# A diffusion block on one core: recurrence units of four channel tiles instead of two, a root taken from the tanh of the half angle, sums of squares moved to ScalarE

## Chip, cores and metric

The kernel runs on one core of a Trainium2 chip. The metric is the device time of one execution in microseconds; the time shown is the median of three runs. A kernel of this kind has five engines that run side by side, each with its own queue of instructions: TensorE (PE, matrix products), VectorE (DVE), ScalarE (ACT), GpSimd (POOL) and SyncE (SP, which here only issues DMA transfers).

## What is computed

A block of width 1024 over 2048 tokens: a mixing phase, a projection with a residual, and a convolutional feed-forward part. The change touches the mixing phase alone. Cut to what matters:

```python
a_r = sigmoid(block_diag(xa, w_a) + b_a)          # 8 heads of 64x64, xa: 512 channels
i   = sigmoid(block_diag(xa, w_x) + b_x)
a   = exp(-8 * a_r * softplus(-lam))
b   = sqrt(1 - a*a) * (i * xa)
h[t] = a[t] * h[t-1] + b[t]                       # forward, and once more backward
ya = gelu(z_gate) * (h_f + h_b)                   # 512 channels
yb = pool_group(z_pool)                           # 256 channels
yc = gmlp_group(z_uv)                             # 256 channels
mix = concat(ya, yb, yc) @ w_out                  # then rmsnorm, gate, residual
out = conv_ffn(...)                               # 1024 -> 5632, 3x3 conv, -> 1024
```

The first states of both directions come from the same recurrence over 256 context tokens.

## The kernel before

Channels lie on the partitions. The 512 recurrent channels are four channel tiles of 128 (the sets P and Q hold two each), the 2048 tokens four chunks of 512. Large products are done in half precision as high and low part, three matmuls for each of eight slices of depth (`mm3`, L356 to L361), so one projection of a channel tile and chunk is 24 matmuls of 128x512. In the trace they are called by what they make: `xa` (input of the recurrence), `gt` (its output gate), `pl` (pooling branch), `uv` (gMLP branch).

A recurrence unit (`lru_units`, L506) takes one direction, one chunk and two channel tiles. For each tile `coeffs` (L440 to L451) issues two f32 matmuls with a 128x128 block-diagonal weight (`rp` L443, `ip` L444; two heads of 64x64 lie on the diagonal, the rest is zero), two sigmoids and a tanh on ACT. `coeffs2` (L453) takes the exponential on ACT, then `combine` (L459 to L463) the square of it and i\*xa on POOL and (q+1)\*t on DVE. `coeffs3` (L465) takes the square root on ACT, `finish_b` (L471 to L473) multiplies on POOL, and `scan` (L475 to L479) runs the recurrence on DVE. So a unit crosses from ACT to POOL and DVE, back to ACT for the root, to POOL, and to DVE. The tiles `lru` hold four arrays of 512 columns and have two buffers. ACT loads a table before each change of function set (`act`, L133 to L141, keeps the sets from mixing).

Forward results are stored to memory (`hfd`, `keep_f` L517). Backward units read them back (`hf`, one buffer) and POOL adds both (`join`, L520 to L523). `gates` (L640 to L648) then applies the gelu of `gt`, multiplies on DVE (L647) and sums squares on DVE (`vsumsq`, L153). `pool_br` (L539) issues `pl`, a chain of DVE adds on tiles `pa` and `pb` and a small f32 matmul `pp` (L535). `gmlp` (L598 to L638) issues `uv`, a normalisation on DVE and POOL, the matmuls `sp` (L623) and the transposes `tp` (L632). `wout_stats` (L684) reads w_out once (`ro`) and sums its squares on DVE; `prep_out` (L695) reads it again (`ro2`) and splits it on DVE into high and low part (L312, L313) for the `wo` matmuls (L878). `mods` (`wm`, L660) makes further modulation rows on DVE.

The order of all this is written by hand: each word of the string `ORDER` (L38 to L43) calls one step, its first letter chosen from the table `run` (L771 to L784): x normalises the next chunk, c is the context recurrence, a the projection `xa`, f and b the recurrence forward and backward, G the gates, g and p one step of gMLP and pooling, m of `wm`, w of w_out, i prepares slots of w_in, L opens the pool of late tiles. A scheduler sorts each engine's instructions by its own estimate of time, with the order of the calls as priority; each engine then runs its list in order.

## Time and profile before

| | |
|---|---|
| median of three runs | 2157.3 us (2153.7 to 2160.75) |
| the profiled execution's own time | 2155.6 us |
| its span | 2153.8 us |
| busy: PE, DVE, ACT, POOL | 2022.0 (94%), 1593.2 (74%), 1194.6 (55%), 610.1 (28%) us |
| mean granted TensorE clock | 0.972 |

The page lists busy time for each engine, 40 equal slices of the span, the DMA queues, the chain of work that ended last (each step followed back to what released it), the costliest groups of instructions and the DMA issues. Below, four further views of the same execution are used: stretches of the span with the busy time of each engine, what an engine waited for, groups of instructions by line and shape, and single instructions in order of time.

### The profile page before, as it was taken

Reading aid. Unit: us, or ns where it says so; the run is one execution under the profiler, and the core shown is the slowest. Engines: PE = TensorE matmul, PEld = TensorE weight load, DVE = VectorE, ACT = ScalarE, POOL = GpSimd, SP = SyncE. Lnnn points to the kernel's source line nnn. Section 1 sums busy time; section 2 is a strip of 40 time slices with the busy share of each in tenths; the row PEclk is TensorE's granted clock in tenths of the full one; section 3 lists DMA queues with packets and bytes.
Section 4 is the critical chain, followed back from the end, with each engine's and each line's share of the span. In section 5 each row is a group of like instructions: output and inputs, shape, how many; then the busy total and the mean of one; then the engine's idle time right before and its main releaser. Section 6 shows DMA issues by size and latency. Waiting matters only on the chain.

```text
span 2153.8 us, 24277 instructions
## 1 busy us (share of the span) xinstructions
PE 2022.0 (94%) x9215; PEld 933.4 (43%) x9215; DVE 1593.2 (74%) x2214; ACT 1194.6 (55%) x1665; POOL 610.1 (28%) x457
## 2 busy tenths in 40 slices
PE   6878989788899998999999999999999999999995
PEld 1433444333455443444444444444444444444442
DVE  5687788999655359978667776867777686777876
...
GB/s 297 183 88 74 69 166 89 180 35 85 135 136 114 79 64 20 130 66 132 89 117 98 79 124 72 108 78 102 94 88 100 74 103 88 100 95 69 40 157 156
DMA packets 73480, 224.78 MB, mean 104 GB/s; under 512 B 7442, under 2 KB 18066, under 8 KB 68498
## 3 DMA queue, kind: packets, MB, share of 16 engines
...
## 4 chain that ended last, share of the span: by engine, by line
PE 55%; DVE 3%; POOL 1%; DMA 1%; ACT 1%; issue 1%; POOLq 0%; SPq 0%; DVEq 0%; ACTq 0%
PE up L359 12%; PE up L360 12%; PE up L361 12%; PE dn L1054 6%; PE dn L1056 6%; PE dn L1055 6%; DVE cv L1011 2%; DMA hT<-accd 1%; POOL hT L1069 0%; DVE hT L1086 0%; DVE hT L1060 0%; DMA wm<-in_wmT_dram 0%; POOL fms L159 0%; PE sct L121 0%; POOL out_dram L1087 0%
## 5 line engine op out<-in xcount | busy, mean ns | idle before, releaser
L1011 DVE SCALAR_TENSOR_TENSOR cv<-z,cols,cv 128x1008 f32<-128x1008 f32 (+3 forms) x704 | 870.4, 1250 | 276.6 <-ACT cv L1005 188.7
L359 PE MATMUL up<-hT,uw 128*128 128x512 f16 x1408 | 534.1, 379 | 2.6 <-ACT z L846 2.6
L361 PE MATMUL up<-hT,uw 128*128 128x512 f16 x1408 | 534.1, 379 | 0.0
L360 PE MATMUL up<-hT,uw 128*128 128x512 f16 x1408 | 534.1, 379 | 0.0
L1071 POOL DMA_DIRECT2D accd<-dd x132 | 114.2, 865 | 704.1 <-ACT dd L1065 697.9
L846 ACT ACTIVATE z<-up,upinv 128x512 f32<-128x512 f32 x176 | 120.5, 685 | 311.2 <-PE up L361 310.8
L1065 ACT ACTIVATE dd<-dn,gdi 128x512 f32<-128x512 f32 x320 | 214.2, 680 | 115.0 <-PE dn L1056 107.5
L1054 PE MATMUL dn<-dw,gs 128*128 128x512 f16 x704 | 267.2, 380 | 7.1 <-ACT dd L1065 5.3
L1055 PE MATMUL dn<-dw,gs 128*128 128x512 f16 x704 | 267.5, 380 | 0.0
L1056 PE MATMUL dn<-dw,gs 128*128 128x512 f16 x704 | 265.8, 380 | 0.0
L360 PEld LDWEIGHTS <-uw 128*128 128x128 f16 x1408 | 137.8, 98 | 167.5 <-issue 3.6
L359 PEld LDWEIGHTS <-uw 128*128 128x128 f16 x1408 | 139.0, 99 | 164.7 <-issue 0.6
L361 PEld LDWEIGHTS <-uw 128*128 128x128 f16 x1408 | 137.8, 98 | 166.5 <-issue 0.6
L832 POOL TENSOR_TENSOR uw<-ur,uw 128x2048 f16<-128x2048 f32 x22 | 89.5, 4070 | 168.9 <-ACT ur L831 168.9
L135 ACT ACT_TABLE_LOAD x77 | 98.8, 1283 | 47.4 <-PE rp L443 28.8
L1005 ACT ACTIVATE cv<-z,cols 128x1024 f32<-128x1024 f32 x88 | 106.0, 1206 | 2.0
L1055 PEld LDWEIGHTS <-gs 128*128 128x128 f16 x704 | 68.8, 98 | 86.8 <-issue 9.5
L1054 PEld LDWEIGHTS <-gs 128*128 128x128 f16 x704 | 72.2, 103 | 78.8 <-issue 0.8
L1056 PEld LDWEIGHTS <-gs 128*128 128x128 f16 x704 | 68.9, 98 | 83.5 <-issue 0.6
L986 POOL TENSOR_TENSOR dw<-dr,dw 128x1024 f16<-128x1024 f32 x22 | 46.4, 2127 | 141.8 <-PE dn L1056 100.3
L150 ACT ACTIVATE junk<-g 128x1024 bf16<-128x1024 f32 x44 | 46.3, 1053 | 59.9 <-DVE g L1019 59.9
L878 PE MATMUL wo<-wo,ysp 128*128 128x512 f16 x256 | 77.1, 383 | 1.0 <-ACT gm L807 1.0
...
## 6 DMA issues: line engine op xcount, KB each, us to landing
...
ur<-in_wup_dram SPq DMA_DIRECT2D x22, 1024.0 KB, 5.6
...
hT<-in_wm_dram SPq DMA_DIRECT2D x8, 1024.0 KB, 14.4
xt<-in_xT_dram SPq DMA_DIRECT2D x8, 1024.0 KB, 7.1
...
```

What stands on the lines that cost most here:

```text
L135: ins = A.activation(out_, in_, func, **kw).ins
L359: T.matmul(ps, wh(k), hh(k), start=(k == 0), stop=False)
L360: T.matmul(ps, wh(k), hl(k), start=False, stop=False)
L361: T.matmul(ps, wl(k), hh(k), start=False, stop=(k == KT - 1))
L846: A.activation(z[:, ab, b * 8:(b + 1) * 8, :], ps.rearrange("p (r x) -> p r x", x=64), AF.Identity, scale=upinv[:, c:c + 1])
L1005: A.activation(t, z[:, ab, r0:r0 + 16, :].rearrange("p r x -> p (r x)"), AF.Identity, bias=col("fcb", c + NP * ab), scale=wt(0, 0))
L1011: V.scalar_tensor_tensor(o, z[:, ab, ya + dy:yb + dy, xa + dx:xb + dx], wt(dy, dx), o, op0=OP.mult, op1=OP.add)
L1054: T.matmul(ps[h], hi, wh, start=i == 0, stop=False)
L1055: T.matmul(ps[h], hi, wl, start=False, stop=False)
L1056: T.matmul(ps[h], lo, wh, start=False, stop=i == n - 1)
L1065: A.activation(d[:, h * CH:(h + 1) * CH], ps[h], AF.Copy, scale=di)
L1071: G.dma_start(accd[t], d, accum_op=OP.add)
```

## The change

Seven edits. (1) A recurrence unit takes all four channel tiles (set A); the table tile `lru` holds three arrays and has four buffers, in a pool of its own. (2) The root is taken from the tanh of the half: with t = tanh(4pr) and a = exp(-8pr), sqrt(1-a\*a) = (1+a)\*sqrt(t). So ACT does sigmoids, tanh, exp and sqrt without waiting for POOL or DVE between them; POOL and DVE follow (i\*xa, (a+1)\*i, i\*sqrt); the square of a on POOL is gone. (3) Each gate matmul of 128x128 becomes two of 64x64 that use the upper and lower half of the partitions of input and output; the weight is loaded by eight transfers of 64x4x64 instead of one of 128x4x4x128. (4) The sums of squares of `gg`, `pa` and `ro` go from DVE to ACT (`sumsq`, L149). (5) The split of w_out goes from DVE (two instructions) to ACT (two) and POOL (one) (`split_ag`, L315 to L319 before). (6) gMLP's output is written over the tile it came from, `gg` has two buffers, not three. (7) `ORDER` is new, with one step F (`fold_ffn`) that ran after the mixing phase before.

Program instructions from before to after: gate matmuls 64 of 128x512 and 16 of 128x256 to 128 of 64x512 and 32 of 64x256; ACT table loads 77 to 44; DVE 2120 to 2073, ACT 1479 to 1494, POOL 462 to 430, SP 312 to 319.

```diff
 ORDER = """
-x1 cP g g cQ x2 a1P f0P a1Q g a2P f0Q x3 g f1P a2Q g f1Q a3P g f2P L a3Q m6
-g i89 f2Q g g i45 m6 f3P g g g g f3Q g g g m6 i67 m6 b3P p p p p
-m6 b3Q G3P p m6 w4 b2P G3Q p m6 w4 b2Q G2P p m6 w2 b1P G2Q p m6 w2 b1Q G1P p
-m6 w2 b0P G1Q m6 w2 b0Q G0P m9 G0Q w9 w9
+x1 cA g g g x2 a1P a1Q f0A g g x3 a2P a2Q f1A g g g a3P a3Q f2A L g g i89 m6 f3A g g g g i45 m6 g g g m6 i67 m6
+b3A p p p G3P m6 p p G3Q m6 w4 b2A p p p p G2P m6 w4 G2Q m6 w2 b1A m6 w2 G1P m6 w2 G1Q m6 w2 F b0A w2 G0P G0Q w9 w9
 """
...
-    gwt = mix.tile([128, 4, 4, 128], F32, name="gwt")
+    gwt = mix.tile([128, 4, 4, 64], F32, name="gwt")
+    HALVES = (slice(0, 64), slice(64, 128))
...
+        V.tensor_scalar(lam, p, -4.0, None, op0=OP.mult)
...
+    def lru_tile(name):
+        return lrup.tile([128, 3, CH], F32, tag="lru", name=name)
...
-        T.matmul(rp[:, :w], gwt[:, j, 2 * d, :], xa, start=True, stop=True)
-        T.matmul(ip[:, :w], gwt[:, j, 2 * d + 1, :], xa, start=True, stop=True)
-        c = lru_tile([128, 4, CH], F32, "lru") if c is None else c
-        r, i, t, q = (c[:, a, :] for a in range(4))
-        act(r[:, :w], rp[:, :w], AF.Sigmoid, bias=col("ba", 4 * d + j))
-        act(i[:, :w], ip[:, :w], AF.Sigmoid, bias=col("bx", 4 * d + j))
-        k = klam[:, 4 * d + j:4 * d + j + 1]
-        act(t[:, :w], r[:, :w], AF.Tanh, scale=k)
-        return r, i, t, q, k
-
-    def coeffs2(cs, xas, w):
-        for c in cs:
-            act(c[0][:, :w], c[0][:, :w], AF.Exp, scale=c[4])
-        for c, xa in zip(cs, xas):
-            combine(c, xa, w)
-
-    def combine(c, xa, w):
-        r, i, t, q, k = c
-        G.tensor_tensor(q[:, :w], r[:, :w], r[:, :w], op=OP.mult)
-        G.tensor_tensor(i[:, :w], i[:, :w], xa, op=OP.mult)
-        V.scalar_tensor_tensor(t[:, :w], q[:, :w], 1.0, t[:, :w], op0=OP.add, op1=OP.mult)
-
-    def coeffs3(cs, w):
-        for c in cs:
-            act(c[2][:, :w], c[2][:, :w], AF.Sqrt, scale=-1.0)
-        for c in cs:
-            finish_b(c, w)
-
-    def finish_b(c, w):
-        i, t = c[1], c[2]
-        G.tensor_tensor(i[:, :w], i[:, :w], t[:, :w], op=OP.mult)
+        for ps, g in ((rp, 2 * d), (ip, 2 * d + 1)):
+            for h in HALVES:
+                T.matmul(ps[h, :w], gwt[h, j, g, :], xa[h], start=True, stop=True)
+        c = lru_tile("lru") if c is None else c
+        r, i, t = (c[:, a, :w] for a in range(3))
+        act(r, rp[:, :w], AF.Sigmoid, bias=col("ba", 4 * d + j))
+        act(i, ip[:, :w], AF.Sigmoid, bias=col("bx", 4 * d + j))
+        act(t, r, AF.Tanh, scale=col("lam", 4 * d + j))
+        return r, i, t, klam[:, 4 * d + j:4 * d + j + 1]
+
+    def coeffs2(cs, xas):
+        for r, i, t, k in cs:
+            act(r, r, AF.Exp, scale=k)
+        for r, i, t, k in cs:
+            act(t, t, AF.Sqrt, scale=-1.0)
+        for (r, i, t, k), xa in zip(cs, xas):
+            G.tensor_tensor(i, i, xa, op=OP.mult)
+            V.scalar_tensor_tensor(i, r, 1.0, i, op0=OP.add, op1=OP.mult)
+            G.tensor_tensor(i, i, t, op=OP.mult)
 
...
-        ts = [lru_tile([128, 4, CH], F32, "lrc") for j in js]
+        ts = [lru_tile("lrc") for j in js]
         cs = [coeffs(j, d, xac[0][:, j, :], LC, ts[j - js[0]][:, :, d * LC:(d + 1) * LC]) for j, d in jd]
-        coeffs2(cs, [xac[0][:, j, :] for j, d in jd], LC)
-        coeffs3(cs, LC)
+        coeffs2(cs, [xac[0][:, j, :] for j, d in jd])
         for (j, d), c in zip(jd, cs):
-            q = c[3]
+            q = c[2]
...
-        cs = [coeffs(j, d, Y[n][:, j, :], CH, bank=b) for j, b in zip(js, (pB, pA))]
-        coeffs2(cs, [Y[n][:, j, :] for j in js], CH)
-        coeffs3(cs, CH)
+        cs = [coeffs(j, d, Y[n][:, j, :], CH, bank=b) for j, b in zip(js, (pB, pA, pB, pA))]
+        coeffs2(cs, [Y[n][:, j, :] for j in js])
         for j, c in zip(js, cs):
-            o = c[3]
+            o = c[2]
...
-                    vsumsq(a[:, 0:CH], yb[n - 1], ysq[:, n - 1, 4 + pt:5 + pt])
+                    sumsq(a[:, 0:CH], yb[n - 1], ysq[:, n - 1, 4 + pt:5 + pt])
...
-            yc = mix.tile([128, 2, 256], F32, tag="yc", bufs=1, name="yc")
+            yc = guvt[:, :, 0:256]
             A.activation(yc, tp_ps.rearrange("p (c t) -> p c t", c=2), AF.Identity)
-            sumsq(guv[0].rearrange("p (c t) -> p c t", c=2), yc, ysq[:, n, 6 + r:7 + r])
+            sumsq(guvt[:, :, 256:512], yc, ysq[:, n, 6 + r:7 + r])
...
-                g = late.tile([128, CH], F32, tag="gg", bufs=3, name="gg")
+                g = late.tile([128, CH], F32, tag="gg", bufs=2, name="gg")
                 act(g, ps, AF.Gelu_apprx_tanh, scale=inv[:, 4 + j:5 + j])
                 V.tensor_tensor(Y[n][:, j, :], g, Y[n][:, j, :], op=OP.mult)
-                vsumsq(g, Y[n][:, j, :], ysq[:, n, j:j + 1])
+                sumsq(g, Y[n][:, j, :], ysq[:, n, j:j + 1])
...
-            vsumsq(r, r, t[:, k:k + 1])
+            sumsq(r, r, t[:, k:k + 1])
...
-        split(s[:, 0, :], s[:, 1, :], r, wosc)
+        split_ag(s[:, 0, :], s[:, 1, :], r, wosc)
...
-    S.dma_start(gwt, gw.rearrange("j p g c -> p j g c"))
+    for j in range(4):
+        for h in HALVES:
+            S.dma_start(gwt[h, j], gw[j, h, :, h])
...
+    lruc = tc.tile_pool(name="lru", bufs=4, side="right")
+    lrup = lruc.__enter__()
```

What the new order looks like at three places. First ACT at chunk 1 backward (`lru<-rp` and `lru<-ip` are sigmoids, `lru<-lru,klam` before is tanh or exp, `lru<-lru` the root). Before, the first of its two units:

```order
L135 ACT_TABLE_LOAD
L135 ACTIVATE lru<-rp,cols 128x512
L135 ACTIVATE lru<-lru,klam 128x512
L135 ACTIVATE lru<-ip,cols 128x512
L135 ACTIVATE lru<-rp,cols 128x512
L135 ACTIVATE lru<-ip,cols 128x512
L135 ACTIVATE lru<-lru,klam 128x512
L135 ACT_TABLE_LOAD
L135 ACTIVATE lru<-lru,klam 128x512 x2
L135 ACT_TABLE_LOAD
L135 ACTIVATE lru<-lru 128x512 x2
L135 ACT_TABLE_LOAD
```

Now the end of its one unit, from the third tile on (`lru<-lru,cols` is the tanh):

```order
L133 ACTIVATE lru<-ip,cols 128x512
L317 ACTIVATE ro_3556<-ro_3556,wosc 128x1024
L316 ACTIVATE wo_3619<-ro_3620,wosc 128x1024
L133 ACTIVATE lru<-lru,cols 128x512
L133 ACTIVATE lru<-ip,cols 128x512
L133 ACTIVATE lru<-lru,cols 128x512
L133 ACT_TABLE_LOAD
L133 ACTIVATE lru<-lru,klam 128x512 x2
L317 ACTIVATE ro_3620<-ro_3620,wosc 128x1024
L133 ACTIVATE lru<-lru,klam 128x512 x2
L133 ACT_TABLE_LOAD
L133 ACTIVATE lru<-lru 128x512 x4
```

Two units with three tables each became one with three; the root follows the exponential directly, and splits of w_out (L316, L317) stand between the sigmoids and the exponentials.

Second, PE at the same place. Before, the gate matmuls of one unit and the first gate projection behind them:

```order
L443 MATMUL rp<-Y_94,gwt 128x512
L444 MATMUL ip<-Y_94,gwt 128x512
L443 MATMUL rp<-Y_94,gwt 128x512
L444 MATMUL ip<-Y_94,gwt 128x512
L359 LDWEIGHTS ws_2022
```

Now the unit of four tiles, with the pooling branch's small matmul in it:

```order
L449 MATMUL rp<-Y_94,gwt 64x512 x2
L449 MATMUL ip<-Y_94,gwt 64x512 x2
L449 MATMUL rp<-Y_94,gwt 64x512 x2
L449 MATMUL ip<-Y_94,gwt 64x512 x2
L449 MATMUL rp<-Y_94,gwt 64x512 x2
L525 MATMUL pp<-pb,pwt 128x512
L449 MATMUL ip<-Y_94,gwt 64x512 x2
L449 MATMUL rp<-Y_94,gwt 64x512 x2
L449 MATMUL ip<-Y_94,gwt 64x512 x2
```

Eight gates of two halves stand together, and the second gate of the third tile is behind `pp`.

Third, POOL from chunk 0 backward to the end of the mixing phase (L462 and L463 are i\*xa, L461 the square, L473 and L465 the product with the root, L523 and L513 the joins). Before:

```order
L462 TENSOR_TENSOR lru<-lru,Y_93 128x512 x2
L461 TENSOR_TENSOR lru<-lru 128x512 x2
L473 TENSOR_TENSOR lru<-lru 128x512
L523 TENSOR_TENSOR Y_93<-lru,hf 128x512
L473 TENSOR_TENSOR lru<-lru 128x512
L523 TENSOR_TENSOR Y_93<-lru,hf 128x512
L462 TENSOR_TENSOR lru<-lru,Y_93 128x512 x2
L461 TENSOR_TENSOR lru<-lru 128x512 x2
L473 TENSOR_TENSOR lru<-lru 128x512 x2
L523 TENSOR_TENSOR Y_93<-lru,hf 128x512 x2
```

Now (L318 is the low part of a w_out tile):

```order
L463 TENSOR_TENSOR lru<-lru,Y_93 128x512 x3
L318 TENSOR_TENSOR wo_3555<-ro_3556,wo_3555 128x1024
L463 TENSOR_TENSOR lru<-lru,Y_93 128x512
L318 TENSOR_TENSOR wo_3619<-ro_3620,wo_3619 128x1024
L465 TENSOR_TENSOR lru<-lru 128x512 x4
L513 TENSOR_TENSOR Y_93<-lru,hf 128x512
L318 TENSOR_TENSOR wo_3724<-ro_3725,wo_3724 128x1024
L318 TENSOR_TENSOR wo_3846<-ro_3847,wo_3846 128x1024
L513 TENSOR_TENSOR Y_93<-lru,hf 128x512
L318 TENSOR_TENSOR wo_3852<-ro_3853,wo_3852 128x1024
L513 TENSOR_TENSOR Y_93<-lru,hf 128x512
L318 TENSOR_TENSOR wo_3858<-ro_3859,wo_3858 128x1024
L513 TENSOR_TENSOR Y_93<-lru,hf 128x512
```

All four products with the root stand ahead of the first join, and four tiles of w_out stand between the joins.

## Rows read from the trace of the kernel before

**Rows 1.** The page, section 4: the chain that ended last, share of the span by line
```profile
PE up L359 12%; PE up L360 12%; PE up L361 12%; PE dn L1054 6%; PE dn L1056 6%; PE dn L1055 6%; DVE cv L1011 2%; DMA hT<-accd 1%; POOL hT L1069 0%; DVE hT L1086 0%; DVE hT L1060 0%; DMA wm<-in_wmT_dram 0%; POOL fms L159 0%; PE sct L121 0%; 
```

**Rows 2.** Stages: from:to and length, busy us by engine (count), granted clock, DMA
```profile
0.00:90.80 90.80, 70.84 (x303) 29.77 (x304) 55.45 (x153) 44.67 (x75) 16.96 (x16) 0.89 0.72 276
90.80:369.90 279.10, 238.48 (x992) 113.64 (x991) 223.51 (x442) 185.32 (x270) 102.32 (x97) 0.93 0.27 92
369.90:474.50 104.60, 87.46 (x334) 37.53 (x334) 98.69 (x173) 51.31 (x64) 45.41 (x32) 0.92 0.37 119
474.50:553.00 78.50, 61.85 (x240) 28.09 (x238) 74.88 (x116) 41.00 (x52) 37.93 (x25) 0.90 0.27 84
553.00:2153.80 1600.80, 1563.32 (x7352) 724.33 (x7352) 1140.68 (x1333) 872.32 (x1205) 407.46 (x288) 0.99 0.43 97
```

**Rows 3.** What PE waited for, 90.8 to 474.5 us: total, times, longest us
```profile
PE tp L632 <- DVE guv L630: 19.2, 8, 6.4
PE pp L535 <- DVE pb L574: 16.1, 4, 6.6
PE rp L443 <- ACT lrc L135: 7.0, 2, 5.3
...
PE pp L535 <- DVE scq L126: 0.5, 1, 0.5
```

**Rows 4.** Instruction groups of POOL and DVE, 90.8 to 553 us: busy us, mean ns, idle before
```profile
L461 POOL TENSOR_TENSOR lru<-lru 128x512 f32<-128x512 f32 x32 | 37.9, 1203 | 14.4 <-ACT lru L135 14.4
...
L463 DVE SCALAR_TENSOR_TENSOR lru<-lru 128x512 f32<-128x512 f32 x32 | 32.0, 1023 | 25.2 <-POOL lru L461 25.1
...
L153 DVE SCALAR_TENSOR_TENSOR gg<-Y 128x512 f32<-128x512 f32 x16 | 15.0, 938 | 0.2
L153 DVE SCALAR_TENSOR_TENSOR ro<-ro 128x1024 f32<-128x1024 f32 x8 | 13.7, 1716 | 0.4 <-DMA ro<-in_wout_dram 0.4
...
L313 DVE SCALAR_TENSOR_TENSOR wo<-ro,wosc,wo 128x1024 f16<-128x1024 f32 x8 | 13.0, 1640 | 0.0
```

**Rows 5.** The same view of ACT
```profile
L135 ACT ACT_TABLE_LOAD x72 | 92.4, 1283 | 46.6 <-PE rp L443 28.8 <-DVE state L514 12.7 <-DMA hfd<-lru 3.8
...
L135 ACT ACTIVATE lru<-rp,cols 128x512 f32<-128x512 f32 x32 | 21.9, 684 | 6.5 <-PE gt L361 3.0 <-issue 1.5 <-DMA hfd<-lru 1.4
...
L135 ACT ACTIVATE lru<-lru 128x512 f32<-128x512 f32 x32 | 19.9, 629 | 42.3 <-DVE lru L463 42.2
...
L150 ACT ACTIVATE ws<-rw 128x1024 bf16<-128x1024 f32 x6 | 6.3, 1052 | 5.5 <-DMA rw<-in_win_dram 5.5
```

**Rows 6.** ACT in order of time, first unit of chunk 1 backward: start, us
```profile
480.75 1.28 ACT L135 ACT_TABLE_LOAD   x1
482.04 1.33 ACT L135 ACTIVATE lru<-lru,klam 128x512 f32<-128x512 f32 x2
...
485.98 1.23 ACT L135 ACTIVATE lru<-lru 128x512 f32<-128x512 f32 x2 [1.30 <-DVE lru L463]
```

**Rows 7.** POOL splits of a weight tile in the front (L319): shortest, median, longest ns
```profile
L319 POOL TENSOR_TENSOR ws<-rw,ws x2: 2123/2126/2129, 53.6 to 60.8; 128x1024 f16<-128x1024 f32 x2
```

**Rows 8.** PE in order of time, the same unit: start, us, count at the end
```profile
474.48 1.02 PE L443 MATMUL rp<-Y,gwt 128*128 128x512 f32 x2
475.33 1.02 PE L444 MATMUL ip<-Y,gwt 128*128 128x512 f32 x2
```

**Rows 9.** POOL in order of time, 490 to 500 us: the joins
```profile
490.91 1.69 POOL L523 TENSOR_TENSOR Y<-lru,hf 128x512 f32<-128x512 f32 x1 [1.22 <-issue]
495.68 1.78 POOL L523 TENSOR_TENSOR Y<-lru,hf 128x512 f32<-128x512 f32 x1 [3.08 <-DMA hf<-hfd]
```

**Rows 10.** What PE waited for, 474.5 to 553.2 us
```profile
PE pp L535 <- DVE pb L574: 7.0, 2, 5.4
PE sct L121 <- DVE gsfmm L297: 4.6, 1, 4.6
```

**Rows 11.** A transfer of the front, 0 to 90.8 us: KB, us to landing
```profile
gwt<-in_gw_dram SPq DMA_DIRECT2D x1, 1024.0 KB, 15.6
```

More of the change, by code (lines that the diff above doesn't have):

```diff
@@ L173, in block_kernel @@
     mix = mixc.__enter__()
-    gwt = mix.tile([128, 4, 4, 128], F32, name="gwt")
-    def lru_tile(shape, dt, name):
-        return mix.tile(shape, dt, tag="lru", bufs=2, name=name)
+    gwt = mix.tile([128, 4, 4, 64], F32, name="gwt")
+    HALVES = (slice(0, 64), slice(64, 128))
+    lru0c = tc.tile_pool(name="lru0", bufs=1, side="right")
+    lru0 = lru0c.__enter__()
     earlyc = tc.tile_pool(name="early", bufs=1)
@@ L196, in block_kernel @@
     wmv = hT.bitcast(F32).rearrange("p a k t -> p (a k t)").rearrange("p (k t) -> p k t", k=KT)
-    brow = lru_tile([2, 2048], F32, "brow")
+    brow = lru0.tile([2, 2048], F32, name="brow")
     lx = load_x(0)
-    r23 = lru_tile([128, 2, 1024], F32, "r23")
+    r23 = lru0.tile([128, 2, 1024], F32, name="r23")
     win_raw = [rawt(f"rw{j}") if j < 2 else r23[:, j - 2, :] for j in range(4)]
@@ L222, in stats_first @@
     def stats_first(xt):
-        acc = early.tile([128, CH], F32, tag="acc", name="acc")
+        acc = early.tile([128, 2, CH], F32, tag="xs", bufs=2, name="acc")[:, 0, :]
         sq = early.tile([128, 2, CH], F32, tag="xs", bufs=2, name="sq")
@@ L442, in coeffs @@
         rp, ip = bank("rp"), bank("ip")
[L443 to L473 removed]
+        for ps, g in ((rp, 2 * d), (ip, 2 * d + 1)):
[16 more added lines that the diff above has]
+            G.tensor_tensor(i, i, t, op=OP.mult)
     def scan(o, c, w, init, rev):
[L476 removed]
+        r, i = c[0], c[1]
         if rev:
@@ L717, in block_kernel @@
         S.dma_start(cr[h], ctxT[:, 4 * h:4 * h + 4, :].rearrange("p k t -> p (k t)"))
-    S.dma_start(gwt, gw.rearrange("j p g c -> p j g c"))
+    for j in range(4):
+        for h in HALVES:
+            S.dma_start(gwt[h, j], gw[j, h, :, h])
     S.dma_start(wst, wsT)
     S.dma_start(gnr, gnorm.to_broadcast([128, 256]))
-    hc = lru_tile([128, 2, 8, LC], F16, "hc")
+    hc = lru0.tile([128, 2, 8, LC], F16, name="hc")
     norm_apply(lambda k: cr[k // 4].rearrange("p (k t) -> p k t", k=4)[:, k % 4, :], LC, gs_c,
@@ L727, in block_kernel @@
     xa_ctx(hc)
+    lru0c.__exit__(None, None, None)
+    lruc = tc.tile_pool(name="lru", bufs=4, side="right")
+    lrup = lruc.__enter__()
     prep_uv([conv0])
@@ L753, in late_open, with fold_ffn @@
         S.dma_start(pwt, pw)
-    late = latec = pwt = None
+    late = latec = pwt = gs_f = sc_f = None
+    def fold_ffn():
+        nonlocal gs_f, sc_f
+        gs_f, sc_f, _ = fold("gsf", col("gpf", 0, 8), mcol[:, 0, 8:16], mcol[:, 0, 16:24])
     def prep_ins(*js):
@@ L769, in block_kernel @@
     ms, ws_, pl = mods(), preps(), pool_br()
-    J = {"P": P, "Q": Q}
+    J = {"P": P, "Q": Q, "A": P + Q}
     run = {
@@ L778, in block_kernel @@
         "L": late_open,
+        "F": fold_ffn,
         "i": lambda *js: prep_ins(*map(int, js)),
@@ L789, in block_kernel @@
     latec.__exit__(None, None, None)
+    lruc.__exit__(None, None, None)
     mixc.__exit__(None, None, None)
@@ L837, in block_kernel @@
     gm2 = row_of("gm2", on_, 0, col("gqm", 0, 8))
-    gs_f, sc_f, _ = fold("gsf", col("gpf", 0, 8), mcol[:, 0, 8:16], mcol[:, 0, 16:24])
     def up(c, z, w, order=(0, 1, 2, 3)):
```

1 line of the change is left out of this document (removed).

## The prediction

> **What bounds the kernel now.** Begin with the chain that ended last [rows 1]: its long entries are the matmuls of the feed-forward part, and the rest of its lines are small. So from the projection on the kernel is bound by PE, and the change touches nothing there. Next the stages [rows 2]: in 553.0 to 2153.8 us PE is busy 1563.3 of 1600.8 us at a granted clock of 0.99. Nothing is to be had there, so I keep its 1600.8 us. The change acts in the 462.2 us between 90.8 and 553.0 us.
>
> There the busy share of no engine says enough, so read what PE waited for. From 90.8 to 474.5 us (383.7 us) thirteen kinds of wait add up to 57.7 us; the largest are the transposes of gMLP behind DVE (19.2 us), the pooling matmul behind DVE (16.1 us) and the context's gate matmuls behind ACT (7.0 us), the smallest 0.5 us [rows 3]. DVE is the engine that is late: in 369.9 to 474.5 us it is busy 98.7 of 104.6 us, more than PE with 87.5 [rows 2].
>
> A wait costs twice, since the granted clock falls with it. The mean is 0.93 in the first stretch and 0.92 in the second [rows 2]. With two levels, 1.2 and 2.4 GHz, a mean of 0.93 is 14% of the time at the lower one, 0.92 is 16%: 39.1 and 16.7 us, 55.8 together. PE was busy 85% and 84% of these stretches, and half of busy time at the low level is lost: 55.8 x 0.85 / 2 = 23.7 us, an estimate, or 0.41 us for each of the 57.7 us of waiting.
>
> From 474.5 to 553.0 us the bound is another one: PE is busy only 61.9 of 78.5 us. Here a chain runs through chunk 1 backward and chunk 0 backward, unit by unit: gate matmuls, ACT, POOL, DVE, back to ACT, POOL, scan, join, gate. DVE is busy 74.9 us of it.
>
> **Part by part.** *Root and units.* The square of a (37.9 us of POOL) goes, and with it the wait of DVE for it (25.2 us), and that of the root for DVE (42.2 us) [rows 4, 5]. ACT loads 33 tables less, by the row 33 x 1.28 = 42.3 us [rows 5]. None of this is PE's own wait, so in the sum it counts only as far as DVE and ACT come earlier where PE waits for them. Each load is over in 1.28 us and the next function starts 0.01 us behind it [rows 6]. The Trainium skill ("ScalarE: Activation LUTs", What ACT_TABLE_LOAD costs) puts a switch at about 2.7 us with a drain, which would make the 33 loads some 88 us; the row disagrees, and the sum would be the same by either, as ACT is not what binds.
>
> *Squares and splits.* The squares of `gg` and `ro` and the low parts of w_out alone take 15.0 + 13.7 + 13.0 = 41.7 us from DVE [rows 4], nearly all of it after 369.9 us. ACT gets 16 and 8 of 512 columns at about 0.68 us (the sigmoid's row), 8 of 1024 at 1.05 us and 16 splits of 1024 that I take at the same: 16 + 8 + 17 = 41 us, as much as the table loads gave back [rows 5]. ACT is busy 277.6 of 462.2 us [rows 2], so this is covered in bulk; where it stands in a queue it is not (second rival). POOL loses 38 us and the context's squares and gets 8 x 2.13 = 17 us [rows 4, 7].
>
> *Waits of PE to 474.5 us.* I go through the 57.7 us. The context start stays (7.0 to about 5.3, its longest wait). The transposes wait for a DVE that is interleaved with scans and with the product that waits for POOL; one such group in place of two for each chunk should halve them, 19.2 to 10. The pooling matmul keeps most, 16 to 13: all its steps now stand between the first two backward units, with joins, scans and `wm` in front, though the squares of `pa` and `ro` are gone. New are about 4.5 us before the gates of chunk 3 forward, as only 48 `uv` matmuls stand between the forward units of chunks 2 and 3, and about 5 us for gMLP's `sp` behind the same; both are estimates by the context's 5.3 us, the one place in the trace where gates wait for ACT. Together 38 us, 19.7 us less. With 0.41 us of clock for each, 8.1 us more.
>
> *Gates in halves.* A gate matmul is two records, and the next gate starts 0.85 us later, so 0.43 us for each record [rows 8]. If both halves run side by side, a gate costs the same 0.85 us; if one after the other, 1.7 us. The trace of before has no matmul of 64 rows, so both ends stand: 0, and the first rival's +37 us. I take 0, plus a loss at each of 9 units (the context's, four forward, four backward): one further start of 0.43 us and, on going in and coming out, the 0.16 us by which a record outlasts its pitch (0.59 against 0.43; 1.02 us for two in the row [rows 8]): 9 x 0.43 = 3.9, rounded up with the second to +4 us, at the worst +7. I take it nearer the lower end because the halves share no partition of input or output. The Trainium skill bears on this twice, and no row here shows either. "TensorE: Matmul & The Clock Gate" (Part 3: Packing small matmuls) says that matmuls at different positions of the array run together and end in program order. "TensorEngine Tiling (Array Packing)" (Key Properties) speaks against the change: to change the tiling mode drains TensorE. By the first page the term is +4, by the second it lies towards the +7, and the forecast would be 2137.
>
> *End of the mixing phase.* b1 of four tiles: a table 1.28, twelve functions of 0.68 (8.2), two tables and four exponentials and roots each (2 x (1.28 + 4 x 0.65) = 7.8): the roots end 17.3 us after ACT's start. Before, the first of two such chains ran from its first gate matmul at 474.48 to the end of its roots at 487.2, 12.7 us [rows 5, 6, 8]. The first join follows at about +21; the joins are 4.8 us apart (1.7 us on POOL, 3.1 us for the one `hf` buffer [rows 9]), so the last is at +35. All four `lru` buffers are then in use, so the sigmoids of chunk 0 come at about +36. Their chain takes 21 us to the first join, 15 for four joins with four low parts of 2.13 us in the gaps [rows 7], and 8 for the last gate, its square and the statistics: +80 against 78.5. I take +1 us, between -8 (PE's waits of 7.0 for pooling and part of the 4.6 for the fold, which F moves, are gone [rows 10]) and +12 (a w_out tile or its square ahead of each of the last joins).
>
> *Front.* The gate weights are 768 KB less at 276 GB/s, -2.8 us at best [rows 2, 11]; at worst the seven added transfers hold the queue half as long again as the one took, +8 us. The stage ends with work behind other transfers, so I take 0. The tile over its source, two buffers of `gg` and the move of `fold_ffn` I cost at nothing: DVE and POOL have room there after the relief; without it each would show at the end of the mixing phase, in the +12.
>
> *Sum.* -19.7 - 8.1 + 4 + 1 + 0 = -22.8 us. Against the profiled execution's 2155.6 us: 2132.8. The median lies 1.7 us above it: **2134 us**.
>
> **Rivals.** *First, slower: the halves run one after the other.* Then a gate costs 0.85 us more at 512 columns, 0.43 at 256: 64 x 0.85 + 16 x 0.43 = 61.3 us. Before chunk 1 backward that is 48 x 0.85 + 6.9 = 47.7, of which about 19, half of the 38 us left to wait, hide; +29. At the end ACT gets a tile every 3.4 us, four in 13.8 rather than 8.2, twice, part of it behind the joins: +8. 2155.6 - 22.8 + 37 = 2169.8, as a median **2171**. It decides as soon as a unit's 16 half matmuls take longer than about 11.5 of the 13.8 us (against 6.9 side by side). For it: the records of before run one behind the other without overlap of starts. Against: they are one position of the array, these are two.
>
> *Second, no change: the gain is given back on ACT and SP.* Squares of `ro` and `pa` and the splits wait in ACT's list, in order, for transfers and POOL; roots and gelus stand behind them. In SP's list a `ro` stands behind an `hf`, which waits for the join before it. If each of four backward units lost about 5 us so, it would be 2155, within 0.3% (6.5 us, about what a measurement tells from no change). For it: the DMA of `hf` already made a join wait 3.08 us [rows 9]. Against: the weights are asked for long before the projection.
>
> *Third, larger gain.* DVE's relief of over 42 us falls where DVE binds (98.7 of 104.6 us [rows 2]), and a POOL with less work keeps DVE less (L463 waits 25.1 us for it [rows 4]). If nearly all waits but the context's and some 10 us of pooling went: 57.7 - 15 = 43, with 17 of clock, less the 5 added: -55, **2100**.
>
> **How the numbers follow.** Forecast 0.52, first rival 0.22, second 0.14, third 0.12. The forecast's own range, with -3/+8 of the front, -8/+12 of the end and +7 for the halves, is about 2118 to 2150. The range for all, 2100 to 2172, takes in both priced ends and leaves out a larger gain and a larger loss. Faster by over 0.3% are the forecast and the third, 0.64; within, 0.15; slower, 0.21.
>
> **What would show it.** Right: gate records of 64 rows that start in pairs, a unit of 16 in about 7 us; PE's waits before chunk 1 backward near 38 us, transposes near 10; a granted clock of 0.95 there; DVE about 40 us less busy; the end of the mixing phase as long as before; from the projection on, 1600.8 us again. Wrong: a unit's gates over 11.5 us, or roots and gelus that wait behind squares and splits on ACT.

## The result and the profile after

The change made the kernel slower: 2175.6 us, median of four runs (2175.1 to 2176.1), against 2158.2 for the kernel before beside it; the ratio is 1.0091, 95% interval 1.0074 to 1.0108. The forecast was 2134, with a range that ended at 2172. The profiled execution has a span of 2173.7 us, 19.9 more than before.

Read the stages first, cut as in [rows 2]: at the first gate matmul of the context, at the place where 192 matmuls of gate projections (`gt`) are left for PE, and at the first matmul of the projection (the second stage is cut at 374 us only to keep the two halves apart). In the change the middle cut is the first gate of chunk 1 backward. In the kernel before it is not: 474.5 us, and with it [rows 6, 8], is the second of the two units of chunk 1, and the first one's gates start at 452.6 us. Columns as in [rows 2]:

```profile
0.00:91.10 91.10, 71.03 (x302) 29.62 (x302) 55.78 (x155) 45.23 (x76) 16.95 (x16) 0.89 0.73 271
91.10:374.00 282.90, 241.46 (x1104) 105.38 (x1103) 205.91 (x418) 162.37 (x259) 93.76 (x74) 0.93 0.24 84
374.00:483.10 109.10, 86.39 (x339) 35.30 (x339) 80.69 (x163) 43.42 (x75) 21.69 (x15) 0.87 0.39 131
483.10:576.30 93.20, 63.43 (x281) 26.80 (x281) 49.13 (x81) 67.96 (x101) 53.53 (x32) 0.84 0.27 89
576.30:2173.70 1597.40, 1562.38 (x7352) 724.14 (x7352) 1139.33 (x1322) 870.15 (x1202) 407.51 (x288) 0.99 0.43 96
```

From the context to the middle cut 392.0 us have gone by where it was 383.7 (+8.3), the end of the mixing phase takes 93.2 where it was 78.5 (+14.7), and the rest 1597.4 where it was 1600.8 (-3.4). Behind the middle cut PE has the same gate projections left in both, but the kernel before has three units of two tiles to go, the change two units of four. Its backward units come later: the first gates of chunk 1 and of chunk 0 were at 452.6 and 491.1 us, and are at 483.1 and 521.7 now. PE in order of time, before:

```profile
452.56 1.02 PE L443 MATMUL rp<-Y,gwt 128*128 128x512 f32 x2
...
491.14 1.02 PE L443 MATMUL rp<-Y,gwt 128*128 128x512 f32 x2
```

And now, chunk 0 (chunk 1 is shown below):

```profile
521.66 1.07 PE L449 MATMUL rp<-Y,gwt 64*64 64x512 f32 x4
```

The granted clock is 0.87 and 0.84 in the two middle stages, where it was 0.92 and 0.90. DVE is relieved as forecast, and by more: 335.7 us busy in the three middle stages, where it was 397.1.

What PE waited for from 91.1 to 483.1 us (total, times, longest), the answer to [rows 3]:

```profile
PE pp L525 <- DVE pb L570: 20.2, 3, 8.8
PE sp L613 <- DVE guv L608: 12.7, 4, 4.9
PE xa L358 <- ACT guv L133: 7.9, 1, 7.9
PE rp L449 <- DVE Y L424: 5.5, 1, 5.5
...
PE sp L613 <- DVE wsc L126: 4.8, 1, 4.8
PE pp L525 <- DVE pb L564: 2.8, 1, 2.8
PE tp L622 <- DVE guv L620: 1.7, 4, 0.8
```

All twelve kinds add up to 63.9 us; they were 57.7 (thirteen kinds). The transposes are down from 19.2 to 1.7 us, more than I hoped. But their wait has moved one step up the same chain, to gMLP's `sp` (12.7 + 4.8 us; 0.9 before), and pooling's `pp` went from 16.1 to 23.0. New is `xa` behind a gelu of ACT, 7.9 us.

And in the end stage, the answer to [rows 10]:

```profile
PE wo L878 <- DVE ysp L311: 25.0, 1, 25.0
PE pp L525 <- DVE pb L570: 4.8, 1, 4.8
```

One wait of 25.0 us stands before the projection. PE has done everything else and has nothing to do until chunk 0 has gone through its unit.

The gates in halves are as forecast. PE in order of time at chunk 1 backward; a count of 4 is two halves of two records each:

```profile
482.81 0.38 PE L360 MATMUL gt<-hT,ws 128*128 128x512 f16 x1
483.12 1.07 PE L449 MATMUL rp<-Y,gwt 64*64 64x512 f32 x4
484.03 1.02 PE L449 MATMUL ip<-Y,gwt 64*64 64x512 f32 x4
484.89 1.02 PE L449 MATMUL rp<-Y,gwt 64*64 64x512 f32 x4
...
490.39 1.02 PE L449 MATMUL ip<-Y,gwt 64*64 64x512 f32 x4
491.35 0.39 PE L358 MATMUL gt<-hT,ws 128*128 128x512 f16 x1
```

A gate starts every 0.86 us, 0.85 before [rows 8], with twice as many matmuls in it. Going in costs 0.31 us from the last `gt` to the first gate, and coming out 0.96 us from the last gate to the next `gt`: about 0.1 us more each than with whole gates, where the same two steps took 0.22 and 0.86 us.

Now two places where PE waits. First DVE ahead of a wait of `sp`, in the unit of chunk 1 forward:

```profile
225.82 2.27 DVE L471 TENSOR_TENSOR_SCAN lru<-lru,state 128x512 f32<-128x512 f32 x1 [2.54 <-POOL lru L465]
...
228.19 2.04 DVE L471 TENSOR_TENSOR_SCAN lru<-lru,state 128x512 f32<-128x512 f32 x1
...
230.33 2.04 DVE L471 TENSOR_TENSOR_SCAN lru<-lru,state 128x512 f32<-128x512 f32 x1
...
232.82 1.25 DVE L471 TENSOR_TENSOR_SCAN lru<-lru,state 128x512 f32<-128x512 f32 x1
...
234.78 0.41 DVE L607 TENSOR_SCALAR guv<-guv,mv,rsv 128x256 f32<-128x256 f32 x1 [0.52 <-POOL rsv L157]
235.23 0.43 DVE L608 TENSOR_TENSOR guv<-guv,gnr 128x256 f32<-128x256 f32 x1
```

DVE waits 2.54 us for POOL, then runs four scans, the first three 2.0 to 2.3 us each, and between them serves gMLP's short normalisation steps one at a time. The last (L608) ends at 235.7, and `sp` starts at 235.8, 4.9 us late. With units of two there were two scans in a row. Ahead of the other long waits of `sp` (2.9, 4.7 and 4.8 us) gMLP's steps stand among four scans too; in the last two, rows of `wm` stand in DVE's list as well.

Second the end: SP's queue, then POOL, then DVE from chunk 0's gates on (PE starts these at 521.7):

```profile
523.86 17.40 SPq L688 DMA_DIRECT2D ro<-in_wout_dram  x4
550.90 0.33 SPq L512 DMA_DIRECT2D hf<-hfd  x1
...
557.65 5.94 SPq L512 DMA_DIRECT2D hf<-hfd  x2
567.58 0.33 SPq L819 DMA_DIRECT2D ur<-in_wup_dram  x1
...
569.48 0.56 SPq L870 DMA_DIRECT2D yr<-ybc  x1
```

```profile
541.94 6.80 POOL L465 TENSOR_TENSOR lru<-lru 128x512 f32<-128x512 f32 x4 [1.03 <-ACT lru L133]
548.70 2.18 POOL L513 TENSOR_TENSOR Y<-lru,hf 128x512 f32<-128x512 f32 x1
550.84 5.56 POOL L318 TENSOR_TENSOR wo<-ro,wo 128x1024 f16<-128x1024 f32 x2
556.37 1.26 POOL L513 TENSOR_TENSOR Y<-lru,hf 128x512 f32<-128x512 f32 x1
...
561.96 1.27 POOL L513 TENSOR_TENSOR Y<-lru,hf 128x512 f32<-128x512 f32 x1
...
566.29 1.26 POOL L513 TENSOR_TENSOR Y<-lru,hf 128x512 f32<-128x512 f32 x1 [0.98 <-DMA hf<-hfd]
```

```profile
569.07 0.48 DVE L311 TENSOR_SCALAR ysp<-Y,ysc 128x512 f16<-128x512 f32 x1 [0.79 <-ACT gg L148]
...
575.57 0.49 DVE L311 TENSOR_SCALAR ysp<-yr,ysc 128x512 f16<-128x512 f32 x1 [5.23 <-DMA yr<-ybc]
```

POOL makes the four products with the root (541.9 to 548.7), then joins at 548.7, 556.4, 562.0 and 566.3, with w_out's low parts between. Joins came 4.8 us apart before [rows 9]; the first two are now 7.7 apart. SP spends 17.4 us on four loads of `ro`, each behind a buffer that POOL has to free (12.5 us in the kernel before). What SP waited for from 350 us on:

```profile
SPq L512 <- POOL Y L513: 32.0, 13, 9.6
...
SPq L688 <- POOL wo L318: 22.4, 6, 7.8
```

In this stage the `hf` of the joins (L512) is not late by `ro`, though it stands behind it: each `hf` waits for the join that frees its one buffer, and leaves as that join ends (the first at 550.90, the join ends at 550.88). Last, SP issues `yr`, the projection's operand, behind the last `hf` and two other loads, at 569.5, 1.9 us after the last join has ended; DVE gets it at 575.6 (5.23 us of waiting), and the projection starts at 576.3. In the kernel before, `yr` left at 541 to 543 us, as the last join ended and 10 us ahead of the projection.

### The profile page after: what moved, and what is told of

It is laid out like the page before. It is cut to its first block, busy times and chain, and to the rows that moved or that the text cites. A ratio compares the mean times of both kernels' runs of the same rounds, so it can differ in the third digit from the quotient of the medians.

```text
span 2173.7 us, 24576 instructions
## 1 busy us (share of the span) xinstructions
PE 2024.7 (93%) x9375; PEld 921.2 (42%) x9375; DVE 1530.8 (70%) x2135; ACT 1189.1 (55%) x1712; POOL 593.4 (27%) x425
## 4 chain that ended last, share of the span: by engine, by line
PE 54%; DVE 4%; POOL 1%; issue 1%; DMA 1%; ACT 1%; POOLq 0%; SPq 0%; DVEq 0%
PE up L358 12%; PE up L359 12%; PE up L360 12%; PE dn L1054 6%; PE dn L1056 6%; PE dn L1055 6%; DVE cv L1011 2%; POOL hT L1069 0%; DMA hT<-accd 0%; DVE hT L1086 0%; DVE hT L1060 0%; DMA wm<-in_wmT_dram 0%; POOL fms L157 0%; PE sct L119 0%; POOL out_dram L1087 0%
## 5 line engine op out<-in xcount | busy, mean ns | idle before, releaser
L1011 DVE SCALAR_TENSOR_TENSOR cv<-z,cols,cv 128x1008 f32<-128x1008 f32 (+2 forms) x704 | 870.9, 1250 | 273.2 <-ACT cv L1005 183.6
L463 POOL TENSOR_TENSOR lru<-lru,Y 128x512 f32<-128x512 f32 x32 | 44.2, 1391 | 141.9 <-ACT lru L133 132.5
```

The source lines that it names most:

```text
L1011: V.scalar_tensor_tensor(o, z[:, ab, ya + dy:yb + dy, xa + dx:xb + dx], wt(dy, dx), o, op0=OP.mult, op1=OP.add)
```

## The experiments

All ratios are against the kernel before on the same chip, with a 95% interval. A change of 0.1% is 2.2 us.

**One part alone in the kernel before.**

The gates in halves:

```diff
-        T.matmul(rp[:, :w], gwt[:, j, 2 * d, :], xa, start=True, stop=True)
+            for h in HALVES:
+                T.matmul(ps[h, :w], gwt[h, j, g, :], xa[h], start=True, stop=True)
```

> The kernel before with one edit: each gate matmul in two 64x64 halves, the gate weights in eight small transfers. Theory (the unit of four is what costs): the halves run side by side, so the time is that of before, 2158 within 6 us, and a gate still costs 0.85 us. Rival (the mode of the array costs at each switch): with 17 groups of gates instead of 9 it shows more here than in the change, slower by 10 us or more.

Measured 2153.4 against 2154.8: 0.9995 (0.9984 to 1.0006). No difference.

The root from the tanh of the half (`coeffs` and `coeffs2` as in the change, but with the four-array tile, and whole gates):

```diff
-            act(c[2][:, :w], c[2][:, :w], AF.Sqrt, scale=-1.0)
+            act(t, t, AF.Sqrt, scale=-1.0)
+            V.scalar_tensor_tensor(i, r, 1.0, i, op0=OP.add, op1=OP.mult)
```

> The kernel before with one edit: the root from the tanh of the half (square on POOL gone, exp and sqrt one after the other on ACT). Units of two, order, squares and splits as before. Theory: the chain of a unit gets shorter and nothing is added, so faster by 8 to 20 us (2138 to 2150). Rival (the waits of PE come from DVE's own load, the chain was covered): within 6 us of 2158.

2152.4: 0.9990 (0.9979 to 1.0000). The rival: the 42.2 us that the root waited for DVE [rows 5] were covered.

Squares and splits:

```diff
-            vsumsq(r, r, t[:, k:k + 1])
+            sumsq(r, r, t[:, k:k + 1])
-        split(s[:, 0, :], s[:, 1, :], r, wosc)
+        split_ag(s[:, 0, :], s[:, 1, :], r, wosc)
```

> The kernel before with one edit: the squares of gg, pa and ro on ACT and the splits of w_out on ACT and POOL. Theory (unit of four): DVE is relieved of some 55 us where it is full, so between no change and 10 us faster. Rival (ACT's list gives the gain back): slower by 10 us or more, with roots and gelus behind squares that wait.

2154.3: 1.0003 (0.9989 to 1.0017). No difference, the lower end of the theory; the rival falls. In the trace PE now waits before the projection for POOL's last low part of w_out; that this takes back what DVE's relief gave was not tested:

```profile
PE wo L878 <- POOL wo L319: 12.1, 1, 12.1
```

**The order and the units.**

The order of the change in the kernel before, each `A` written as `P` and `Q`:

```diff
-x1 cP g g cQ x2 a1P f0P a1Q g a2P f0Q x3 g f1P a2Q g f1Q a3P g f2P L a3Q m6
...
+x1 cP cQ g g g x2 a1P a1Q f0P f0Q g g x3 a2P a2Q f1P f1Q g g g a3P a3Q f2P f2Q L g g i89 m6 f3P f3Q g g g g i45 m6 g g g m6 i67 m6
+b3P b3Q p p p G3P m6 p p G3Q m6 w4 b2P b2Q p p p p G2P m6 w4 G2Q m6 w2 b1P b1Q m6 w2 G1P m6 w2 G1Q m6 w2 b0P b0Q w2 G0P G0Q w9 w9
```

> The kernel before with one edit: the order of the change, each unit of four written as two of two (the step F, which it lacks, left out). Theory (the order costs, whatever the units and engines): slower by 15 us or more, 2170 to 2185. Rival (order and the other edits only hurt together, by ACT's and POOL's fuller lists at the end): within 8 us of before.

2186.5: 1.0141 (1.0123 to 1.0159), slower than the change itself. The order alone costs some 30 us with the old units.

The changed kernel with `A` written as `P` and `Q`:

```diff
-x1 cA g g g x2 a1P a1Q f0A g g x3 ...
+x1 cP cQ g g g x2 a1P a1Q f0P f0Q g g x3 ...
-b3A p p p G3P m6 ... b2A ... b1A ... b0A w2 G0P G0Q w9 w9
+b3P b3Q p p p G3P m6 ... b2P b2Q ... b1P b1Q ... b0P b0Q w2 G0P G0Q w9 w9
```

> The changed kernel with one edit: in its order each unit of four tiles is written as two units of two, one behind the other (cP cQ, f0P f0Q and so on); four buffers, halves, root, squares and the rest of the order stay. Theory (unit of four): scans come two at a time, the last chain is shorter; 2175.6 falls by 12 us or more. Rival (the order of pooling, gates and w_out steps costs, not the unit): within 6 us of 2175.6.

2180.6: 1.0120 (1.0101 to 1.0140). My first theory, that the unit of four costs, falls: with units of two the time is no better, by these figures a little worse.

The changed kernel with the old order, `F` at its end:

```diff
-b3A p p p G3P m6 p p G3Q m6 w4 b2A p p p p G2P m6 w4 G2Q ...
+m6 b3Q G3P p m6 w4 b2P G3Q p m6 w4 b2Q G2P p m6 w2 b1P G2Q ...
+m6 w2 b0P G1Q m6 w2 b0Q G0P m9 G0Q w9 w9 F
```

> The changed kernel with one edit: the order of before, in units of two (F at its end). Halves, root, four buffers, squares and splits of the change stay. Theory (order): back to before or better, 2140 to 2157. Rival (the other edits hurt together): stays above 2165.

2167.6: 1.0062 (1.0044 to 1.0080). About half of the loss in units of two comes back, and 0.62% stays, with the old order and with three parts that cost nothing alone.

New order up to the first backward unit, old order from there:

```diff
 x1 cP cQ g g g x2 a1P a1Q f0P f0Q g g x3 a2P a2Q f1P f1Q g g g a3P a3Q f2P f2Q L g g i89 m6 f3P f3Q g g g g i45 m6 g g g m6 i67 m6
-b3P b3Q p p p G3P m6 p p G3Q m6 w4 b2P b2Q p p p p G2P m6 ...
+b3P p p p p m6 b3Q G3P p m6 w4 b2P G3Q p m6 w4 b2Q G2P p m6 ...
```

> The changed kernel in units of two with the new order up to the first backward unit and the order of before from there (F at its end). Theory (it is the backward half: all pooling between the first two backward units, gates not lagging behind): within 6 us of the run with the whole old order. Rival (the forward half costs as much, where the units stand together and gMLP waits): 8 us or more slower than that run.

2167.1: 1.0057 (1.0041 to 1.0073), the same as with the whole old order. The forward half of the order costs nothing in units of two; the backward half costs the difference of 1.0120 and 1.0057, 0.63% or 13.6 us. (`F` goes back to the end with it; moved by itself, in the faster version further below, it makes no difference.)

**Which part of the backward order.** Three edits of the change, in units of four:

```diff
-b3A p p p G3P m6 p p G3Q m6 w4 b2A p p p p G2P m6 w4 G2Q m6 w2 b1A m6 w2 G1P m6 w2 G1Q m6 w2 F b0A w2 G0P G0Q w9 w9
+b3A p p p m6 b2A G3P p m6 G3Q p m6 w4 b1A G2P p p m6 w4 G2Q p m6 w2
+b0A G1P p m6 w2 G1Q m6 w2 F w2 G0P G0Q w9 w9
```

> The changed kernel in units of four with a new backward order: each backward unit is called ahead of the gates of the chunk before it, and pooling is spread over three chunks, so that 192 gate projections and no longer 96 stand behind the last unit on PE. Theory (PE ran out of work behind the last unit): PE's wait of 25 us before the projection falls below 12, and the time to 2160 or less. Rival (the chain of units with four buffers and one hf buffer sets the end, wherever the gates stand): 2170 to 2180.

2160.4: 1.0027 (1.0016 to 1.0038). That gives back 0.64%, and PE's wait before the projection is 6.2 us. Two things are changed in it, so each alone; pooling spread:

```diff
+b3A p p p p G3P m6 p G3Q m6 w4 b2A p G2P m6 p w4 G2Q m6 w2 b1A p m6 w2 G1P p m6 w2 G1Q m6 w2 F b0A w2 G0P G0Q w9 w9
```

> The changed kernel with one edit of its order: the nine pooling steps spread over the backward half (four, one, one, one, one, one) as in the kernel before; backward units stay behind the gates of the chunk before. Theory (pooling all between the first units takes PE's cover from the last ones): PE's wait before the projection falls from 25 us to 15 or less, the time to 2160 to 2168. Rival (it is where the units stand against the gates): within 5 us of 2175.6.

2178.0: 1.0108 (1.0092 to 1.0123). Nothing comes back, PE's wait is still 21.5 us, and my theory of pooling falls. Units ahead of the gates (steps of `m` and `w` move along with them, and `F` now stands behind the last unit):

```diff
+b3A p p p m6 p p b2A G3P m6 G3Q w4 p p p p b1A G2P m6 w4 G2Q m6 w2 b0A G1P m6 w2 G1Q m6 w2 F w2 G0P G0Q w9 w9
```

> The changed kernel with one edit of its order: each backward unit called ahead of the gates of the chunk before it; pooling stays before the third backward unit as in the change. Theory (pooling's place): within 5 us of 2175.6. Rival (the units' place): 2160 to 2166, as with both edits (2160.4).

2161.2: 1.0028 (1.0015 to 1.0040). It is the units' place. The trace shows how: PE starts chunk 0's gates at 492.7, not 521.7, about where the kernel before started them (491.1), with the gates' projections of chunk 1 still to do, and the projection starts at 561.5, not 576.3. What PE waits for in that stage:

```profile
PE sct L119 <- DVE yt L855: 11.6, 1, 11.6
...
PE wo L878 <- DVE ysp L311: 5.1, 1, 5.1
```

**Squares and splits, taken back.** The changed kernel with the squares of `gg`, `pa`, `ro` and the splits on DVE again:

```diff
-                sumsq(g, Y[n][:, j, :], ysq[:, n, j:j + 1])
+                vsumsq(g, Y[n][:, j, :], ysq[:, n, j:j + 1])
-        split_ag(s[:, 0, :], s[:, 1, :], r, wosc)
+        split(s[:, 0, :], s[:, 1, :], r, wosc)
```

> The changed kernel with one edit undone: the squares of gg, pa and ro and the splits of w_out back on DVE, and so no part of w_out's preparation on ACT or POOL. Theory now (backward order 13 us, the moved squares and splits most of the other 13): 2160 to 2168. Rival (ACT and POOL have room, moving back only loads DVE again): 2175 or more.

2171.1: 1.0068 (1.0053 to 1.0083), between the two: 0.23% comes back, at the edge of the noise (the two intervals overlap). The end of the mixing phase hardly gets shorter, 91.3 us for 93.2, with DVE busy 76.2 of them where it was 49.1. The same in the old order:

> The changed kernel with the order of before (units of two) and the squares and splits back on DVE; left of the change are halves, root, lru buffers, the gMLP output over its source and two gg buffers. Theory (squares and splits make the 12.8 us that the run with the old order lost to before): 2152 to 2159. Rival (the reused gMLP tile and the two gg buffers make them): 2163 or more.

2162.9: 1.0035 (1.0022 to 1.0048), 0.27% back from 1.0062, so neither theory is the whole of it. The same with the units ahead (the order of the run with 2160.4 us):

> Units of four with each backward unit called ahead of the gates of the chunk before it, and the squares and splits back on DVE. Theory (both causes add): below 2154, faster than before; 2148 to 2154. Rival (with the backward order mended, ACT's fuller list no longer stands in the way): 2158 to 2164, as without this edit.

2171.3: 1.0072 (1.0056 to 1.0087), slower by 0.45% than 1.0027. Both theories fall. The traces point to DVE. From chunk 0's gates to the projection it is busy 35.4 of 70.0 us with squares and splits on ACT and POOL, and 61.3 of 75.0 us with them on DVE (columns as above):

```profile
492.00:562.00 70.00, 54.40 (x248) 24.32 (x246) 35.44 (x69) 48.62 (x72) 34.05 (x20) 0.91 0.31 102
```

```profile
501.00:576.00 75.00, 57.52 (x251) 25.32 (x249) 61.31 (x119) 25.67 (x36) 17.93 (x12) 0.91 0.33 98
```

And from 430 us on PE waits 12.2 us for DVE's pooling chain in the first, 29.7 us in the second:

```profile
PE pp L526 <- DVE pb L571: 12.2, 2, 8.9
```

```profile
PE pp L526 <- DVE pb L565: 20.1, 3, 11.6
PE pp L526 <- DVE pb L571: 9.6, 1, 9.6
```

So to move squares and splits off DVE costs 5 us in one order and gives 10 in another.

**The reused tile.** ACT's waits for transfers in the changed kernel (engine, line, waited for: total, times, longest), and in it with the old order:

```profile
ACT ro L148 <- DMA ro<-in_wout_dram: 23.3, 5, 18.6
...
ACT guv L133 <- DMA ybc<-guv: 17.0, 2, 10.3
```

```profile
ACT guv L135 <- DMA ybc<-guv: 15.5, 3, 8.6
```

A gelu of gMLP waits for the store of the output that now lies in its tile. With the old order and a tile of its own for that output, and three `gg` buffers:

```diff
-            yc = guvt[:, :, 0:256]
+            yc = lrup.tile([128, 2, 256], F32, tag="yc", bufs=1, name="yc")
-                g = late.tile([128, CH], F32, tag="gg", bufs=2, name="gg")
+                g = late.tile([128, CH], F32, tag="gg", bufs=3, name="gg")
-    lruc = tc.tile_pool(name="lru", bufs=4, side="right")
+    lruc = tc.tile_pool(name="lru", bufs=3, side="right")
```

> The changed kernel with the order of before (units of two), the gMLP output in a tile of its own again and three gg buffers; squares and splits stay on ACT and POOL, lru has three buffers. Theory (squares and splits cost): 2163 to 2168, as without this edit. Rival (the reused tile makes gMLP's next gelu wait for the store, the run with the old order shows 15.5 us of that on ACT): 2154 to 2159.

2160.7: 1.0026 (1.0016 to 1.0036). The rival. With the tile alone, two `gg` buffers as in the change:

> The changed kernel with the order of before (units of two) and the gMLP output in a tile of its own; two gg buffers and squares and splits stay. Theory (the store of the reused tile holds the next gelu): 2160 to 2163, as with three gg buffers added (2160.7), and ACT's waits for that store gone. Rival (the third gg buffer made the difference): 2166 to 2168.

2159.4: 1.0017 (1.0008 to 1.0026), 0.45% or 9.7 us back from 1.0062. It is the tile, not `gg`, and ACT's wait for that store is gone from the trace. The two units of chunk 3 backward start at 334.2 and 367.0 us, not 343.0 and 375.7: the loss lies in the forward half, where gMLP runs. Both runs also have three `lru` buffers for four; what that does by itself was not measured.

In units of four, with four `lru` buffers, a tile of its own was not run.

**A faster version.** The kernel before with halves, root and, in the memory that the halves free, two `hf` buffers:

```diff
-        hf = late.tile([128, CH], F32, tag="hf", bufs=1, name="hf")
+        hf = late.tile([128, CH], F32, tag="hf", bufs=2, name="hf")
```

> The kernel before with the edits that cost nothing alone: halves, root, and two hf buffers in the memory that the halves free; its order, units of two, squares on DVE. Theory (the end of before is bound by the chain of units, joins 4.8 us apart): faster than before by 4 to 10 us, 2145 to 2151. Rival (the root's 1.3 us or so for each unit and the second buffer are covered): within 4 us.

2149.1: 0.9973 (0.9963 to 0.9982), the time as the theory had it. Where it comes from is less clear: joins now stand 2.8 to 3.8 us apart, but the end of the mixing phase takes 76.0 us for 78.5, less than half of the gain. With the step `F` ahead of chunk 0:

```diff
-m6 w2 b0P G1Q m6 w2 b0Q G0P m9 G0Q w9 w9
+m9 m9 w2 F b0P G1Q m6 w2 b0Q G0P m9 G0Q w9 w9
```

> The faster version (before with halves, root and two hf buffers, 2149.1) with the step F moved ahead of the last chunk, with the modulation rows it needs. Theory (PE's wait of 4.8 us for the fold stands just before the projection, whose operand comes later anyway): within 3 us of 2149. Rival (the fold on DVE is in the last chain): faster by 3 to 6 us.

2149.2: 0.9971 (0.9957 to 0.9984), no difference. And with the squares of `gg` and `pa` on ACT, but `ro` and the splits left on DVE:

```diff
-                vsumsq(g, Y[n][:, j, :], ysq[:, n, j:j + 1])
+                sumsq(g, Y[n][:, j, :], ysq[:, n, j:j + 1])
```

> The same with the squares of gg and pa on ACT too (ro and the splits stay on DVE, so nothing of it waits for a transfer). Theory (in the order of before DVE is full in the last stage, and the squares harm only where ACT's list then waits for transfers or POOL): 2 to 6 us faster than without. Rival (covered, as in the run with all squares and splits alone): within 2 us.

2143.1: 0.9938 (0.9920 to 0.9956), 0.62% faster than the kernel before and the best of all. Its stages, columns as above:

```profile
0.00:88.90 88.90, 70.13 (x302) 29.73 (x302) 52.83 (x153) 46.05 (x78) 18.28 (x16) 0.90 0.77 280
88.90:468.50 379.60, 329.81 (x1463) 139.23 (x1462) 295.93 (x603) 242.91 (x358) 113.51 (x95) 0.94 0.32 101
468.50:539.70 71.20, 58.73 (x261) 24.82 (x262) 55.06 (x85) 47.99 (x76) 26.63 (x18) 0.93 0.27 84
539.70:2136.70 1597.00, 1561.73 (x7352) 724.00 (x7352) 1140.15 (x1329) 872.69 (x1204) 407.70 (x288) 0.99 0.44 97
```

The end of the mixing phase takes 71.2 us, where it was 78.5, with DVE busy 55.1 of them where it was 74.9; up to there it takes 379.6 where it was 383.7. This execution was the fastest of its six (2138.5 us), so its stages show more than the gain of the median.

## Why the prediction was wrong

The time lies outside the range and on the other side of no change: -22.8 us forecast, +19.9 in the span. Some 33 us of the miss lie ahead of the middle cut, in the waits of PE and their clock, and some 13 in the end of the mixing phase. By the steps:

- *Projection and later, untouched:* right, 1597.4 for 1600.8 us.
- *Gates in halves, +4, at the worst +7:* right, at its lower end. 0.86 us for a gate, about 0.1 us at each change of mode, no difference alone. The first rival is refuted, and that its 2171 came near is luck: halves that ran one after the other would have shown 1.7 us. The Trainium skill's "TensorE: Matmul & The Clock Gate" (Part 3: Packing small matmuls) says that they run together, and the trace agrees. By the Trainium skill's "TensorEngine Tiling (Array Packing)" (Key Properties) a change of mode drains the array; the 0.1 us are all that the trace has of it.
- *Root, 33 tables less:* the edits came as counted, and I was right that none of it was PE's own wait. Alone it is worth at most 0.2%.
- *Waits of PE to 474.5 us, 57.7 to 38, with 8.1 us of clock:* wrong, they are 63.9, and the granted clock, which I had at 0.95, was 0.93 and then 0.87. This is the step that missed by most. DVE was relieved as forecast, and PE's waits for it did not fall with that. The transposes fell, but I let their wait go away where it only moved to the step ahead of it: the normalisation in front of `sp` stands in DVE's list among four scans that come together. I had 5 us for it, it took 17.5. Pooling, where I had 13, took 23.0, and `xa` waited 7.9 us for a gelu, where I had nothing. In units of two, with the same order, `sp` waited 6.4 us, the transposes 12.1 and `pp`, up to the projection, 31.5 (27.8 in the change), so four scans in a row are one way into these waits and not the only one; how much each weighs was not told apart.
- *The tile over its source, costed at nothing:* wrong, and it was the one edit of which I said least. A gelu now waits until the store from its tile has landed, 15.5 us in all on ACT in the old order, where the edit costs 9.7 us (1.0062 to 1.0017). In the change ACT shows the same wait (17.0 us), but its price there was not measured.
- *End of the mixing phase, +1 between -8 and +12:* wrong, +14.7. I had priced the chain of chunks 1 and 0 at 80 us and then set it against 78.5, as if it ran from the same start. It did not: the 78.5 us begin at the second unit of chunk 1 and hold three units of two. From the first gate of chunk 1 the kernel before took 100.4 us (452.6 to 553.0), and the change takes 93.2. So from there on the change is not slower; its chain starts 30.5 us later, with less of PE's work left beside it. That lateness is what the sum left out. The run with the units ahead starts chunk 0 at 492.7 us and gives 0.63% back. In the change itself chunk 0's gates came 38.5 us after chunk 1's (I had 36), their first join 27.0 us later (I had 21), the last join ended 18.9 us on (I had 15), and from there it was 8.7 us (I had 8) in which `yr` landed behind everything on SP. The sum was thus short by 13 us. Ten of them lie in two places, by the trace: on ACT, where four splits (4.6 us) stood among chunk 0's sigmoids and exponentials, and on POOL, where low parts of w_out stood between the joins. That the splits are the cause isn't shown: with them back on DVE this stage still took 91.3 us.
- *Squares and splits, covered in bulk:* wrong by some 5 us here (1.0091 to 1.0068, at the edge of the noise). The second rival had this, with one of its places right (ACT behind `ro`, 23.3 us), the other not (at the end no `hf` was late by SP's `ro`), and its price of 20 us too high. How much of the 5 us is ACT's wait was not told apart. Alone in the kernel before the edit costs nothing, and the squares of `gg` and `pa` alone, in the faster version, gain.

The forecast's own range was added up wrongly too: its terms give 2119 to 2157, not 2118 to 2150. The time lies outside either.

The parts add up: backward order 0.63%, tile 0.45%, squares and splits 0.27%, units of four -0.29% (from 1.0120 to 1.0091, whose intervals overlap), 1.06% for the 0.91% measured; halves and root, 0.05% and 0.10% faster alone, would make up the rest. Each is measured in other surroundings, tile and splits in the old order, so the sum is a check and not a proof. The backward order was the largest, and in the prediction it had no term of its own. I took it as given while I priced the units.

What stays open: why the order in the kernel before costs some 30 us and in the changed one 12 to 14; and what the waits ahead of the middle cut would be without each edit. That units of four are no worse than units of two in that order fits the units' place: two of two stand there 3.5 us apart (chunk 0 at 523.5 and 527.0 us).
